# Two instruction streams in a fixed TensorE order for the token mixing of a hybrid decoder

## The chip, the cores and the metric

The kernel runs on one core of one Trainium2 chip. The metric is the device time of one execution in microseconds: 3290.15 us is the median of three runs of the kernel before (3289.18 to 3293.43). The engines are PE (TensorE), DVE (VectorE), ACT (ScalarE), POOL (GpSimd) and SP (SyncE, which issues DMAs).

## The reference

One step of a decoder of two layers for 512 prompt tokens and 8 sample sequences of 8 tokens, 576 tokens in all, width 1024. All in fp32. Cut to what matters:

```
def run_trunk(x, ...):
    for l in range(DEPTH):                       # 2 layers
        x = layer_norm(ALPHA*x + 0.5*swiglu(x, ffn1_w_in, ffn1_w_out))
        mix, st = token_mixing(x, ...)
        x = layer_norm(ALPHA*x + mix)
        x = layer_norm(ALPHA*x + 0.5*swiglu(x, ffn2_w_in, ffn2_w_out))

def token_mixing(h, ...):
    pa, pb, pc, pm, pg = split(h @ w_in)         # one input projection for all branches
    oa = rwkv7_branch(pa)        # 8 heads x 64: a state per head, updated token by token
    ob = pool_branch(pb)         # causal windows of 2, 4, 8, 16
    oc = delta_branch(pc)        # 4 heads x 128: gated delta rule in chunks of 64 tokens
    om = memory_attention(pm)    # 256 memory tokens
    gates = sigmoid(pg)          # 4 x 1024
    merged = sum_i gates_i * (o_i @ w_branch_i)
    return merged @ w_out

# delta rule, by chunk of 64 tokens (the kernel brings the rwkv rule to the same form):
tmat = inverse(eye + strict_lower(...))          # unit triangular, 64 x 64
def step(s, ...):                                # one chunk after another
    v_new = u_i - w_i @ s
    o = qd_i @ s + a_i @ v_new
    s = s * exp(gl_i) + kd_i.T @ v_new
```

## The kernel before

**Dense products.** Features lie on the partitions, tokens on the free axis, in two halves of 288. A weight block of 128 columns is loaded raw by SP's DMA queue, cast to fp32r by ACT (line 232, the high part) and the rest taken by DVE (line 234, the low part); a product of one 128x128 block with 288 tokens is three matmuls (high-high, low-high, high-low, line 248). Eight blocks give 24 matmuls into one PSUM tile. `ffn` does only such products. PSUM tiles of dense products have two buffers each of tags `mm` and `mg` and one of `mf`; all small products use three buffers of the pool `pb`.

**Mixing.** Each layer runs four rwkv pairs of heads (p = 0 to 3, `rwkv_prep`, `rwkv_chain`, `rwkv_out`), then two delta pairs (q = 0, 1, `delta_pair`). A pair has a *preparation* (projections; elementwise work on DVE and ACT; token-by-token matrices `pt` or `pdm` on PE), an *inverse* (`inverse64`: 31 columns of two DVE instructions each, lines 614 and 616, after a transpose at line 608 and before two at 621 and 627; PE then multiplies in `py` and `pd`; the sample group's 8x8 blocks by seven steps `px`) and a *chain* of eight chunks. A rwkv chunk is `pr` on PE, `rhs` on DVE, `psa` on PE, `VS` on ACT, `pu` on PE, `S` on DVE, and the next chunk needs `S`; `pyc` is the output. A delta chunk is `pdk` and `pdq`, `drhs`, `pdz`, `z`, `pdo` and `pdu`, `S`. The sample group has steps of its own, in rwkv laid between the chunks, in delta after them.

**What sets the order.** Every engine runs its instructions in one order, which a list scheduler sets before the run from the program's order and its costs. Dense work that no chain needs yet (pooling, attention, gates `pgt` and branch products `pbr`) is the generator `fill_steps`; `advance` takes steps of it at places given by `ORDER`, `PLAN`, `RWKV_EVERY` and `DELTA_EVERY`, and the scheduler then moves pieces of it into the gaps of PE. It does so matmul by matmul:

```
            if k % self.tk == self.tk - 1 and self.started:
                self.advance(self.fill_gen, 1)
```

stands between the columns of the inverse.

Of the kernel before, what the change touches and what calls it, by code (L numbers as in the profile page):

```python
# [8 lines left out]
F32 = mybir.dt.float32  # L9
# [6 lines left out]
P = 128  # L16
D = 1024
DEPTH = 2
SEQ = 512
NS = 8          # sample sequences  # L20
LS = 8          # tokens of each
# [4 lines left out]
NC_ = 9         # chunks of 64 tokens: 8 of the prompt, one of the sample group  # L26
# [24 lines left out]
# rows of 128 parameters, in two groups that one transpose each brings onto the partitions  # L51
# [4 lines left out]

# how the work that fills the tensor engine's gaps in the token mixing is laid between the rest: its order at first
# (P: pooling and attention, G: gates of the first merge), how many steps of it go where, and how many columns of an
# inverse lie between two steps
ORDER = "P" * 11 + "GP" * 16  # L60
PLAN = (12, 0, 4, 0, 12, 8, 0, 0, 2, 0, 4, 4, 0, 2)
RWKV_EVERY, DELTA_EVERY = 3, 8


class Decoder:
    def __init__(self, tc, ctx, ins, outs):
# [12 lines left out]
        self.ptag = "mm"  # L79
        self.norm = None  # L80
        self.started = False
# [10 lines left out]
    def dense(self, tag, name):  # L92
        return self.pm.tile([P, HT], F32, tag=tag, name=name)

    def fill(self, name):
        return self.pm.tile([P, 512], F32, tag="mg", name=name)
# [14 lines left out]
    def tri(self, t, strict, block=None):  # L111
        """t[s, j] (square in the last two dims of a [n, n] tile): 1 where s <= j (s < j if strict) else 0."""
# [5 lines left out]
    def blockdiag(self, t, b):  # L118
        """zero outside the b x b diagonal blocks of t [n, m]."""
# [8 lines left out]
    def constants(self):  # L128
# [11 lines left out]
        # inclusive upper triangles, by chunk of 64 and by sequence of 8  # L140
# [6 lines left out]
        # seqmask[t, b] = 1 where token t (mod 64) belongs to sequence b  # L147
# [3 lines left out]
        # masks of the RWKV token x token matrices [s | s, t strict | t inclusive]  # L151
# [10 lines left out]
        # 0 where s <= t else NEG: [128 = (h, s), 2 kinds, 64]  # L162
# [17 lines left out]
        # 0 at the first token of a chunk or sequence, else 1  # L180
# [6 lines left out]
        # 1 / (t + 1)  # L187
# [170 lines left out]
    def out_norm(self, units, X, which, lag, ahead, final=False):  # L358
# [7 lines left out]
        def step(i, s):  # L366
# [4 lines left out]
            if kh == 0:  # L371
                ps[s] = self.dense(("mm", "mg")[s], "po")
# [461 lines left out]
    def rwkv_chain(self, l, p, parts):  # L834
# [33 lines left out]
        for _ in sample:  # L868
            pass
# [736 lines left out]
```

## Time and profile before

| | |
|---|---|
| median of three runs | 3290.15 us |
| span of the profiled execution | 3291.1 us |
| PE busy | 3164.5 us, 96% |
| PE weight loads busy | 2886.2 us, 88% |
| DVE busy | 1896.7 us, 58% |
| ACT busy | 1276.8 us, 39% |
| POOL busy | 581.2 us, 18% |

The profiled execution lies within 1 us of the median, so its span can stand for the time. A matmul record begins when the array takes the instruction, and its modelled end reaches into the next ones, so a busy PE is not a PE that does useful work all the time: a record is also lengthened while the array changes from one tile shape to another. The shape stands in the timeline's rows: `128*128` is a product that uses all rows and columns of the array, `64*64`, `128*64` or `32*32` one that uses a part. Waits of PE are listed by what ended them.

### The profile page before, as it was taken

What the parts mean: (1) busy time and instruction counts of PE and PEld (TensorE: products, weight loads), DVE (VectorE), ACT (ScalarE), POOL (GpSimd) and SP (SyncE); (2) the same over time, 40 slices, a digit from 0 to 9 for tenths busy, and PEclk for the clock granted to TensorE, in tenths of its full rate; (3) what the DMA queues carried; (4) which work ended last, traced back from release to release, by engine and by line L of the source; (5) the groups of instructions that cost most, each with busy time, mean ns of one, the idle gap of its engine ahead of it and who ended that gap; (6) DMA issues with size and microseconds to landing.
All of it is one profiled execution on the core that took longest, in us unless ns stands there. A gap on an engine that the chain in (4) does not pass through costs nothing. (4 is left out here: it accounts for less than half of the span.)

```text
span 3291.1 us, 62683 instructions
## 1 busy us (share of the span) xinstructions
PE 3164.5 (96%) x24736; PEld 2886.2 (88%) x24736; DVE 1896.7 (58%) x4205; ACT 1276.8 (39%) x3015; POOL 581.2 (18%) x898
## 2 busy tenths in 40 slices
PE   7999999999999999999999999998999999999998
PEld 7999887688888799999999998776888797989998
DVE  5336676465677656733663376675475786475336
ACT  4323544434434233432343244444345342343324
POOL 2002311111110014400330032111111100152004
PEclk8999899999999899999999999999999998999999
DMA  4223331142233233332333232312322232323222
GB/s 137 80 84 96 87 111 44 41 118 55 60 83 78 57 105 91 91 87 80 88 103 87 81 107 72 105 51 55 102 58 61 67 99 64 98 85 97 84 81 77
DMA packets 509908, 271.96 MB, mean 83 GB/s; under 512 B 45897, under 2 KB 500141, under 8 KB 509613
## 3 DMA queue, kind: packets, MB, share of 16 engines
q1 hardware_dynamic: 509612, 267.95, 29.0%
q8 instruction: 194, 3.18, 0.4%
q14 instruction: 102, 0.83, 0.1%
HBM read 248.12 MB, written 19.76 MB: 81 GB/s over the span
## 5 line engine op out<-in xcount | busy, mean ns | idle before, releaser
L234 DVE TENSOR_TENSOR w<-raw,w 128x512 fp32r<-128x512 f32 (+1 forms) x824 | 604.7, 739 | 385.2 <-ACT w L232 378.0
L232 ACT CAST w<-raw 128x512 fp32r<-128x512 f32 (+1 forms) x824 | 501.6, 615 | 608.8 <-PE po L248 236.4
L248 PE MATMUL pp<-X,w 128*128 128x288 f32 x3552 | 550.9, 307 | 11.1 <-DVE X L262 5.5
L248 PEld LDWEIGHTS pp<-X,w 128*128 128x128 f32 x3552 | 495.1, 193 | 40.1 <-issue 15.3
L248 PE MATMUL pgt<-X,w 128*128 128x288 f32 x3072 | 500.9, 309 | 5.1 <-ACT th__12080 L1484 2.1
L248 PEld LDWEIGHTS pgt<-X,w 128*128 128x128 f32 x3072 | 435.1, 193 | 32.6 <-issue 13.9
L248 PE MATMUL pg<-X,w 128*128 128x288 f32 x3072 | 441.8, 297 | 10.2 <-DVE X L262 6.1
L248 PE MATMUL pu<-X,w 128*128 128x288 f32 x3072 | 437.4, 297 | 0.0
L248 PEld LDWEIGHTS pg<-X,w 128*128 128x128 f32 x3072 | 419.7, 189 | 15.7 <-DVE X L262 9.6
L248 PEld LDWEIGHTS pu<-X,w 128*128 128x128 f32 x3072 | 420.9, 190 | 0.6
L248 PE MATMUL po<-H,w 128*128 128x288 f32 x3072 | 413.9, 296 | 0.0
L248 PEld LDWEIGHTS po<-H,w 128*128 128x128 f32 x3072 | 409.4, 188 | 1.3
L248 PE MATMUL pbr<-O,w 128*128 128x288 f32 x1344 | 227.6, 308 | 12.9 <-ACT w L232 4.1
L248 PEld LDWEIGHTS pbr<-O,w 128*128 128x128 f32 x1344 | 190.9, 191 | 27.9 <-issue 7.3
L276 POOL TENSOR_TENSOR T<-T,m 128x288 f32<-128x288 f32 x48 | 48.0, 1029 | 925.7 <-ACT m L297 925.4
L433 DVE TENSOR_TENSOR h<-h,pu 128x288 f32<-128x288 f32 x128 | 58.0, 453 | 259.2 <-PE pu L248 259.1
L261 ACT CAST H<-h 128x288 fp32r<-128x288 f32 x128 | 55.2, 431 | 189.5 <-DVE h L433 189.4
L432 ACT ACTIVATE h<-pg 128x288 f32<-128x288 f32 x128 | 52.7, 411 | 172.8 <-PE pg L248 172.8
L248 PE MATMUL po<-mh,w 128*128 128x288 f32 x768 | 109.0, 302 | 9.2 <-DVE T L281 9.2
L248 PEld LDWEIGHTS po<-mh,w 128*128 128x128 f32 x768 | 105.6, 193 | 11.4 <-DVE T L281 6.9
L614 DVE TENSOR_TENSOR it<-W,iu 128x60 f32<-128x60 f32 (+24 forms) x372 | 97.7, 263 | 9.2
L353 POOL TENSOR_TENSOR T<-T,off 128x288 f32<-128x288 f32 x96 | 83.4, 900 | 91.5 <-ACT off L348 65.0
(1018 smaller groups left out, 3747.8 us busy)
## 6 DMA issues: line engine op xcount, KB each, us to landing
raw<-in_w_in_dram SPq DMA_DIRECT2D x280, 256.0 KB
raw<-in_ffn_w_in_dram SPq DMA_DIRECT2D x272, 256.0 KB
raw<-in_ffn_w_out_dram SPq DMA_DIRECT2D x160, 256.0 KB
raw<-in_w_branch_dram SPq DMA_DIRECT2D x48, 256.0 KB
raw<-in_w_out_dram SPq DMA_DIRECT2D x48, 256.0 KB
oraw<-od SPq DMA_DIRECT2D x28, 288.0 KB
kraw<-in_mem_w_kv_dram SPq DMA_DIRECT2D x16, 256.0 KB
kvr<-in_cache_mem_k_dram SPq DMA_DIRECT2D x16, 256.0 KB
```

What stands on the lines that cost most here:

```text
L232: nc.scalar.copy(w[:, 0, :m], raw)
L234: low.tensor_sub(w[:, 1, :m], raw, w[:, 0, :m].bitcast(F32))
L248: self.nc.tensor.matmul(ps, w[:, wp, d, :], X[k][:, part, sl], start=first and k == 0 and q == 0, stop=last and k == n - 1 and q == 2)
L261: nc.scalar.copy(out[:, 0, sl], src)
L276: nc.gpsimd.tensor_sub(t, t, self.stat[s]['m'])
L353: nc.gpsimd.tensor_add(T[j], T[j], off)
L432: nc.scalar.activation(h, pg, AF.Silu)
L433: nc.vector.tensor_mul(h, h, pu)
L614: nc.vector.tensor_mul(w, d[:, :r, k:k + 1].to_broadcast([P, r, m]), u[:, k + 1:, k].unsqueeze(1).to_broadcast([P, r, m]))
```

## The change

The order of PE in the mixing is written out by hand (`manual_schedule` for PE alone); DVE, ACT and POOL are still ordered by the scheduler. Preparation, inverse and chain are generators now that yield at the places where PE would wait; the number that they yield is a credit in matmuls, and `feed` takes dense work for it in pieces of twelve matmuls (`mms_steps`), the next pair's projections or the delta gates first (`urgent`). A credit of 8 stands for one hop of a chain, 2 x 8, 7 x 8 and 5 x 8 for longer waits; what a piece takes too much is taken off the next credit.

In the chain, products of one tile shape stand together: `pyc`'s part with the state comes with `pr`, its other part with `pu`, the own-chunk output `pdo` of delta one chunk later with the next `pdz`; the sample group's steps are put beside chunks' products of their own shape (`wide`, `solve`, `deep`; `state`, `solve`, `update`). The 8x8 inverse takes four steps of six products in place of seven steps. Attention's softmax runs two behind its scores, the two halves of `rwkv_out` go together, the delta gates are projected during the inverse, fill weights use the tag `wm` alone, and all dense PSUM tiles have one tag of four banks.

```diff
-ORDER = "P" * 11 + "GP" * 16
-PLAN = (12, 0, 4, 0, 12, 8, 0, 0, 2, 0, 4, 4, 0, 2)
-RWKV_EVERY, DELTA_EVERY = 3, 8
+HOP = 8
+COLUMNS = 2
+PIECE = 12
...
-        self.pm = pool("pm", 2, space=ps)
+        self.pm = pool("pm", 4, space=ps)
...
+    def mms_steps(self, ps, unit, X, sl, then):
+        n, per = len(unit), PIECE // 3
+        for k in range(0, n, per):
+            m = min(n, k + per)
+            self.mms(ps, unit[k:m], X[k:m], sl, k == 0, m == n)
+            if m == n:
+                then()
+            yield 3 * (m - k)
...
     def inverse64(self, U, at):
...
+        last = self.inverse8(U, at, W)
         for k in range(31):
...
-            if k % self.tk == self.tk - 1 and self.started:
-                self.advance(self.fill_gen, 1)
+            if k % COLUMNS == COLUMNS - 1:
+                if k % (2 * COLUMNS) == COLUMNS - 1:
+                    next(last, None)
+                yield HOP - 1
...
-        for k in range(7):
-            px = self.bank("px")
-            for h in range(2):
-                r = slice(at(h), at(h) + 64)
-                a, b = (U(h)[:, 8], x[r]) if k < 6 else (x[r], U(h)[:, 8])
-                nc.tensor.matmul(px[r, :64], a, b, start=True, stop=True)
-            x = self.scr.tile([P, 64], F32, tag="r64", name="ix", bufs=3) if k < 6 else W[:, 8]
-            nc.vector.tensor_sub(x, self.id2, px[:, :64])
...
+    def inverse8(self, U, at, W):
...
+        ps = products("px", (u, on(self.id2)))
+        nc.scalar.copy(a, ps[:, :64])
+        nc.vector.tensor_sub(b, self.id2, ps[:, :64])
+        yield
+        ps = products("px2", (on(a), u), (u, on(a)))
+        nc.scalar.copy(c, ps[:, :P])
+        nc.vector.tensor_add(a, self.id2, ps[:, :64])
+        yield
+        ps = products("px3", (on(b), on(a)), (on(c[:, 0:64]), on(c[:, 64:128])))
+        nc.vector.tensor_copy(w[:, 0:128], ps[:, :P])
+        yield
+        ps = products("px4", (on(b), on(a)))
+        nc.vector.tensor_add(W[:, 8], a, ps[:, :64])
+        yield
...
     def rwkv_prep(self, l, p, front, wx, lr):
...
+        yield 2 * HOP
         for sl in HALVES:
             ps = self.bank("pss")
...
+        yield 7 * HOP
         MA = [self.slot(f"MA{h}", F32, [P, NC_, 2, 64]) for h in range(2)]
...
     def rwkv_chain(self, l, p, parts):
...
+            if S is not None:
+                for h in range(2):
+                    nc.tensor.matmul(py[R[h], :64], S[R[h]], KR[R[h], c, 1], start=True, stop=False)
             nc.vector.tensor_copy(rhs, pr[:, :64])
+            sample_step("wide")
+            yield HOP
             self.rwkv_solve(parts, c, rhs)
-            py, pu = self.bank("pyc"), self.bank("pu")
+            sample_step("solve")
+            yield HOP
+            pu = self.bank("pu")
...
-                if S is not None:
-                    nc.tensor.matmul(py[R[h], :64], S[R[h]], KR[R[h], c, 1], start=True, stop=False)
...
-            next(sample, None)
-        for _ in sample:
-            pass
+            sample_step("deep")
+            yield HOP
...
     def delta_pair(self, l, q, sc):
...
-        self.advance(self.fill_gen, PLAN[8 + 3 * q])
+        yield 2 * HOP
...
+        yield HOP
         for c0, m in ((0, 5), (5, 4)):
             pd = self.bank("pdec")
...
+        yield 2 * HOP
         MA = self.slot("dMA", F32, [P, NC_, 2, 64])
...
+            if c % 3 == 2:
+                yield HOP
...
-        self.advance(self.fill_gen, PLAN[9 + 3 * q])
-        self.tk = DELTA_EVERY
-        DT = self.inverse64(lambda h: MA[R[h], :, 0], lambda h: 64 * h)
+        self.urgent = gates()
+        DT = yield from self.inverse64(lambda h: MA[R[h], :, 0], lambda h: 64 * h)
...
+        yield 5 * HOP
         for c0 in range(0, NC_, 4):
             pt = self.bank("pto")
...
-    def advance(self, steps, n):
-        for _ in range(n):
-            self.started = True
-            if next(steps, self) is self:
+    def feed(self, want):
+        self.credit += want
+        while self.credit > 0:
+            n = None
+            if self.urgent:
+                n = next(self.urgent, None)
+                if n is None:
+                    self.urgent = None
+            if n is None:
+                n = next(self.dense_work, None)
+            if n is None:
+                self.credit = 0
                 return
+            self.credit -= abs(n)
...
     def mixing(self, l):
...
-        self.advance(fill, 1000)
+        with self.tc.manual_schedule(engines={mybir.EngineType.PE}):
+            for want in work:
+                self.feed(want)
+            for _ in self.dense_work:
+                pass
```

Three places of PE's order follow; in a row stand the line, the operation, the tile written and the tiles read, the shape of the result and how many stand together. Line 248 before is line 250 after.

PE before, one rwkv chunk of the first pair (`pp` is dense work, `psa` the solve, `pu` the state's update, `pyc` the output; `S` is the state):

```order
L846 MATMUL pr<-S_5498,KR 64x64
L847 MATMUL pr<-VS,MA_4377 64x64
L846 MATMUL pr<-S_5498,KR 64x64
L847 MATMUL pr<-VS,MA_4378 64x64
L248 MATMUL pp<-X,w 128x288 x3
L830 MATMUL psa<-rhs,W 64x64 x2
L248 MATMUL pp<-X,w 128x288 x3
L854 MATMUL pu<-VS,KN 64x64 x2
L858 MATMUL pyc<-KR,S_5498 64x64
L859 MATMUL pyc<-MA_4377,VS 64x64
L858 MATMUL pyc<-KR,S_5498 64x64
L859 MATMUL pyc<-MA_4378,VS 64x64
```

PE after, a chunk of the same chain:

```order
L250 MATMUL pp<-X,w 128x288 x12
L911 MATMUL pr<-S_5173,KR 64x64
L912 MATMUL pr<-VS,MA_4484 64x64
L911 MATMUL pr<-S_5173,KR 64x64
L912 MATMUL pr<-VS,MA_4485 64x64
L916 MATMUL pyc<-KR,S_5173 64x64 x2
...
L250 MATMUL pp<-X,w 128x288 x12
L886 MATMUL psa<-rhs,W 64x64 x2
L886 MATMUL psa<-r_5205,W 64x64 x2
L926 MATMUL pu<-VS,KN 64x64 x2
L929 MATMUL pyc<-MA_4484,VS 64x64
L929 MATMUL pyc<-MA_4485,VS 64x64
```

Twelve dense matmuls stand ahead of `psa` and ahead of the next `pr`, where three stood; between `psa` and `pu` stood three, and nothing but a sample step's `psa` stands there now; `pyc` with the state has moved up to `pr`. Over the whole program the dense runs are 596 before and 370 after, counted in this order.

PE before, preparation of the first pair, from the last projection of the decay (`pz`, `pa`) over the norms (`pss`) to the matrices (`pt`):

```order
L248 MATMUL pp<-X,w 128x288 x8
L740 MATMUL pa<-wx,lr 128x288
L248 MATMUL pp<-X,w 128x288 x32
L758 MATMUL pss<-yg,b_94 128x288 x2
L248 MATMUL pp<-X,w 128x288 x39
L1298 MATMUL ppool<-pbo,pw 128x288 x2
L248 MATMUL pp<-X,w 128x288
...
L248 MATMUL pp<-X,w 128x288 x34
L786 MATMUL pt_4379<-KR,KB 128x128 x4
```

PE after, the same stretch:

```order
L792 MATMUL pa<-wx,lr 128x288
L250 MATMUL pp<-X,w 128x288 x24
L804 MATMUL pss<-yg,b_94 128x288 x2
L250 MATMUL pp<-X,w 128x288 x48
L837 MATMUL pt_4486<-KR,KB 128x128 x4
```

Between `pa` and `pt` stood 109 dense matmuls, and 72 stand there now.

PE before, preparation of the first delta pair, from the transposes of queries and keys (`ptq`, `ptk`) on:

```order
L1098 MATMUL ptk_10002<-ident,dk 128x128
L248 MATMUL pgt<-X,w 128x288 x22
L248 MATMUL pbr<-O,w 128x288 x6
L248 MATMUL pp<-X,w 128x288
L248 MATMUL pgt<-X,w 128x288 x2
L1106 MATMUL ptv_10020<-ident,dv 128x128 x4
L1097 MATMUL ptq<-ident,dq 128x128 x2
```

PE after, the end of the same transposes and the way to the matrices (`pdm`):

```order
L1187 MATMUL ptk_9822<-ident,dk 128x128
L1195 MATMUL ptv_9828<-ident,dv 128x128
L250 MATMUL pgt<-X,w 128x288 x12
L1217 MATMUL pdec<-dec,b_94 128x320
L1217 MATMUL pdec<-dec,b_94 128x256
L250 MATMUL pgt<-X,w 128x288 x12
L1230 MATMUL pdm<-dk 64x64
```

From the first `ptq` to the first `pdm` stood 55 dense matmuls and stand 24; they have gone from between the transposes. From the last `pt` or `pdm` to the first `py` of an inverse, the six pairs of a layer had 132, 113, 79, 179, 178 and 160 of them (841) and have 96, 108, 72, 48, 108 and 108 (540), beside other fill work.

## Rows read from the trace of the kernel before

**Rows 1.** The page: span, busy time of engines, granted clock by slice.

```profile
span 3291.1 us, 62683 instructions
...
PE 3164.5 (96%) x24736; PEld 2886.2 (88%) x24736; DVE 1896.7 (58%) x4205; ACT 1276.8 (39%) x3015; POOL 581.2 (18%) x898
...
PEclk8999899999999899999999999999999998999999
```

**Rows 2.** Waits of PE: us in total, times, longest.

```profile
PE ppt L1397 <- DVE prob L1318: 14.1, 6, 5.9
...
PE py L635 <- DVE iy L621: 7.4, 3, 3.6
...
PE pt L786 <- DVE KB L773: 2.9, 2, 1.5
```

**Rows 3.** Chain of waits, in order of time: start us, us, what.

```profile
2844.07 3.20 PE pgt L248 x24
```

**Rows 4.** Timeline of PE, one rwkv chunk: start us, us, what, count.

```profile
506.29 0.33 PE L830 MATMUL psa<-rhs,W 64*64 64x64 f32 x4
506.55 0.67 PE L248 MATMUL pp<-X,w 128*128 128x288 f32 x3
507.15 0.36 PE L854 MATMUL pu<-VS,KN 128*64 128x64 f32 x4
507.44 0.33 PE L858 MATMUL pyc<-KR,S 64*64 64x64 f32 x2
507.70 0.33 PE L859 MATMUL pyc<-MA,VS 128*64 128x64 f32 x2
```

**Rows 5.** Timeline of ACT, the same chunk.

```profile
506.67 0.46 ACT L832 ACTIVATE VS<-psa 64x64 f32<-64x64 f32 x2 [2.30 <-PE psa L830]
```

**Rows 6.** Timeline of PE, preparation of the second rwkv pair.

```profile
526.05 0.75 PE L740 MATMUL pa<-wx,lr 64*128 64x288 f32 x2
...
532.08 1.24 PE L758 MATMUL pss<-yg,b 128*128 128x288 f32 x4
...
537.75 5.84 PE L248 MATMUL pp<-X,w 128*128 128x288 f32 x42
545.04 1.92 PE L786 MATMUL pt<-KR,KB 64*128 64x128 f32 x14 [1.45 <-DVE KB L773]
```

**Rows 7.** Timeline of DVE, the same stretch.

```profile
528.08 1.40 DVE L744 TENSOR_TENSOR_SCAN e<-cont,e 128x256 f32<-128x256 f32 x2
...
534.32 3.74 DVE L760 RECIPROCAL yg<-yg 128x576 f32<-128x576 f32 x1
...
544.25 1.53 DVE L773 TENSOR_TENSOR KB<-pa,e 64x576 f32<-64x576 f32 x2
```

**Rows 8.** Groups by line, DVE, the inverses: busy us, mean ns; idle.

```profile
L614 DVE TENSOR_TENSOR it<-W,iu 128x60 f32<-128x60 f32 (+24 forms) x372 | 97.7, 263 | 9.2
L616 DVE TENSOR_TENSOR W<-W,it 128x60 f32<-128x60 f32 (+24 forms) x372 | 82.8, 223 | 9.1
```

**Rows 9.** Timeline of DVE, the inverse of the second rwkv pair.

```profile
553.40 1.97 DVE L608 STREAM_TRANSPOSE iu<-cp 128x1024 f32<-128x1024 f32 x1
...
574.96 0.65 DVE L621 STREAM_TRANSPOSE iy<-W 128x256 f32<-128x256 f32 x1
575.64 1.80 DVE L627 STREAM_TRANSPOSE W<-iy 32x256 f32<-32x256 f32 x4
```

**Rows 10.** Timeline of PE, first delta pair's preparation.

```profile
902.99 0.27 PE L1097 MATMUL ptq<-ident,dq 128*128 128x128 f32 x1
```

**Rows 11.** Timeline of DVE, the same preparation.

```profile
922.31 0.35 DVE L1140 SCALAR_TENSOR_TENSOR dMA<-pdm,dcs,dec 128x128 f32<-128x128 f32 x1
```

**Rows 12.** Timeline of PE, third rwkv pair's preparation: the long wait.

```profile
658.02 0.48 PE L1397 MATMUL ppt<-ident,prob 128*128 128x128 f32 x1 [5.88 <-DVE prob L1318]
658.15 4.19 PE L248 MATMUL pgt<-X,w 128*128 128x288 f32 x16
```

**Rows 13.** Stretches: us, busy of PE, PEld, DVE, ACT, POOL, granted clock.

```profile
655.00:662.00 7.00, 3.98 (x17) 3.97 (x17) 6.97 (x12) 0.00 (x0) 0.00 (x0) 0.55 0.15 42
```

More of the change, by code (lines that the diff above doesn't have):

```diff
@@ L953, in rwkv_out, with rwkv @@
             self.stash(p, y, sl)
-    def rwkv(self, l, fill=None):
+        yield HOP
+    def rwkv(self, l):
         wx, lr, front = self.rwkv_common(l)
-        front = self.rwkv_front(l, 0, front)
+        front, steps = self.rwkv_front(l, 0, front)
+        for _ in steps:
+            pass
         self.sc = self.delta_scalars(l)
+        yield 0
         for p in range(4):
-            parts = self.rwkv_prep(l, p, front, wx, lr)
-            self.advance(fill, PLAN[2 * p])
+            parts = yield from self.rwkv_prep(l, p, front, wx, lr)
@@ L1163, in delta_pair, with sample_step @@
+        group = sample()
+        wanted = next(group)
+        def sample_step(kind):
+            nonlocal wanted
+            if wanted == kind:
+                wanted = next(group, None)
         S = [None, None]
-        for c in range(8):
-            if c:
+        before = None
+        for c in range(9):
+            if 0 < c < 8:
                 pk, pq = self.bank("pdk"), self.bank("pdq")
@@ L1267, in pool @@
             for k in ((0, 1), (2,), (3,), ())[j]:
-                rows(k)
-                yield
+                yield from rows(k)
             w = 2 << j
@@ L1381, in attention, with scores @@
         nc.scalar.copy(KT, pt.rearrange("p (q m) -> p q m", q=2))
+        yield -4
+        PT, po, behind = {}, {}, []
+        def scores(p, h, g):
+            ps = self.fill("psc")
+            for d in range(2):
+                t = (2 * g + d) * P
+                nc.tensor.matmul(ps[:, d * 256:(d + 1) * 256], Q[R[h], p, t:t + P], KT[R[h], p],
+                                 start=True, stop=True)
+            pr = tile("prob", [P, 2, 256])
+            self.softmax(ps.rearrange("p (k m) -> p k m", k=2), pr)
+            behind.append((p, h, g, pr))
@@ new lines, in transposed @@
+        def transposed():
+            p, h, g, pr = behind.pop(0)
+            if g == 0:
+                PT[p, h] = tile("PT", [P, 2, 512])
+            pt = self.fill("ppt")
+            for m in range(2):
+                for d in range(2):
+                    nc.tensor.transpose(pt[:, (2 * m + d) * P:(2 * m + d + 1) * P], pr[:, d, m * P:(m + 1) * P],
+                                        self.ident)
+            nc.scalar.copy(PT[p, h][:, :, g * 256:(g + 1) * 256], pt.rearrange("p (m t) -> p m t", m=2))
+            return p, h, g
@@ L1494, in early @@
                     for s in range(2):
[L1495 to L1509 removed]
+                        yield from gate(j, s, self.M[j // 2][:, j % 2, HALVES[s]])
+            early = early()
+            for k in first:
+                yield abs(k)
+                if k < 0:
+                    yield next(early, 0)
+            yield from early
         for j in range(8):
[L1511 to L1513 removed]
+            if first is None:
+                for s in range(2):
+                    yield from gate(j, s, self.half("th_", "xf"))
             if j == 0:
```

462 lines of the change are left out of this document (257 added, 205 removed).

## The prediction

> **What bounds the kernel now.** I read the page first: PE is busy for 3164.5 of 3291.1 us, DVE for 58% of it [rows 1]. So PE bounds the kernel, and what is not useful on PE is of three kinds: idle time (3291.1 - 3164.5 = 126.6 us), stretches at half clock (the 8 and 9 tenths in the clock's line [rows 1]), and the time in which the array changes between tile shapes, which counts as busy. The list of waits comes next: the largest in the mixing are waits for softmax, inverse and preparation on DVE, and none is a DMA [rows 2]. The longest single wait, 5.9 us, stands where the order had put a transpose of the attention in front of the dense work [rows 2, 12]. The chain of waits gives the price of dense work: 24 matmuls in 3.20 us, 0.133 us each [rows 3]. The timeline of one rwkv chunk shows the third kind [rows 4]: three dense matmuls between `psa` and `pu` are worth 0.40 us by that price, and from `psa` to `pu` go 507.15 - 506.29 = 0.86 us. The rest, 0.46 us, is the way out of the small shape and back, with the issue of four `psa` in it. From `pu` over the first `pyc` to the second stand 0.29 and 0.26 us for four and two matmuls of 64 columns, a step each time that the shape changes.
>
> **What it removes.** The count of matmuls hardly changes; the dense runs fall from 596 to 370. Each run costs the way in and out once. Seen from the dense run alone (506.55 to 507.15, less 0.40) it is 0.20 us, with `psa` 0.46 us [rows 4]; I take 0.35, since most of the 0.46 is not the issue of four matmuls. 226 runs fewer give 79 us (45 to 104). In the chunk, `pu`, `pyc`, `pyc`, `pyc`, `pyc` change the shape four times before; after it `pr` and `pyc` with the state have one shape, `psa` too, and `pu` with the other `pyc` one. Three steps of 0.26 us in 56 of 64 chunks (the first of a chain has no state) are 44 us [rows 4]; the matmuls themselves still issue, and the bare `psa` to `pu` is a new change, so I take 30 (0 to 44). The 8x8 inverse has four steps in place of seven; its returns are in the 226. Of the idle 126.6 us [rows 1] about 55 go, since all waits in the mixing are counted anew below; three of them alone are 14.1 + 7.4 + 2.9 = 24 us [rows 2], so 24 to 80. Together 164 us (69 to 228).
>
> **What it adds: waits at places where the cover is smaller than the chain beside it.** The order of PE is fixed either way; what counts is how much work stands between the two ends of each dependency. Behind an instruction that waits, all dense work waits too.
>
> *Preparation, rwkv.* From `pa` at 526.05 [rows 6] DVE does scan, reciprocal (3.74 us alone) and products until `KB` ends at 544.25 + 1.53 = 545.78 [rows 7]: 19.7 us, with a few weights' and softmax instructions of other work between, so some 16.5 of its own. After, PE has between the same ends 72 x 0.133 = 9.6 us of dense work, `pss` 1.24, `pa` 0.75 [rows 6] and two returns of 0.35: 12.3 us for the first pair. (The second and third pairs have fewer dense matmuls and other fill in their place, near the same sum; the fourth has more.) The wait is 4.2 to 7.4 us; I take 6 for three pairs and 2 for the fourth, 20 a layer, 40 us in all (26 to 55). Before, 109 dense matmuls covered it to 2.9 us in all [rows 2].
>
> *Inverse.* The columns cost (97.7 + 82.8) / 12 = 15.0 us on DVE [rows 8], and the transposes 1.97 + 0.65 + 1.80 [rows 9]: 19.5 us bare. With other DVE work between it took 577.44 - 553.40 = 24.0 us in the trace [rows 9]. PE's cover falls from 841 dense matmuls a layer to 540, or from 18.6 to 12.0 us for one inverse; with the other fill, transposes and returns beside them I put it at 19 us. So the wait at `py` is 0.5 us if DVE does nothing else, 5 us if it does what it did; the changed DVE order has as much other work there as before, and for the first pair more (the pooling sums). I take 5.5 for each of twelve, 66 us (6 to 100). This is the largest and least certain term. In the trace of before it is 7.4 [rows 2], already taken off.
>
> *Hops without work.* A credit of 8 paid by pieces of 12 leaves each third hop bare, and in 46 of 64 chunks it is the one from `psa` to `pu`. There ACT's two instructions run from 506.67 to 507.13, 0.38 after `psa` starts [rows 5]; `pu` starts at 507.15. Of the 0.86 us about 0.2 is PE's own issue and a change of shape, so a bare hop idles 0.65 us: 30 us (20 to 40). For the bare hops elsewhere (`pu` to `pr`, `pdz` to `pdu`) I take 0.4 us at about 45 places, 18 us (0 to 30), each being shorter by what PE issues in it.
>
> *Preparation, delta.* From the first `ptq` at 902.99 [rows 10] to the first `dMA` at 922.31 [rows 11] ACT and DVE need 19.3 us, of which 3 or 4 are weights and merge. PE had 55 dense matmuls up to `pdm`. After it has 24 (3.2 us), 27 transposes, `pdec` and two returns, 8 to 9 us. The wait is 8 to 11 us; four times 10.5 are 42 us (28 to 46). For the norm ahead of `pto`, where 48 dense matmuls (6.4 us) stand beside a like series of ACT instructions, I take 3 us each, 12 us (0 to 25).
>
> Together 40 + 66 + 30 + 18 + 42 + 12 = 208 us (80 to 296).
>
> One PSUM tag of four banks in place of two of two has the same room; fill weights on `wm` alone have four buffers, and the dense runs in which they are used are not longer, so both are at 0 (-5 to +10: if a low part's subtraction queues on DVE behind columns of the inverse, dense work waits for it, as a `pbr` would). The half clock of before stays in the sum. Outside the mixing nothing changes.
>
> **Sum.** 3291.1 - 164 + 208 = 3335 us for the profiled execution, which stands 1 us above the median; I predict 3335. What the hops don't use of the dense work isn't lost: it runs after the last chain without waits, but it can't cover anything there.
>
> **The rivals.**
>
> *The cover is enough, faster.* If DVE does the chain's instructions first and the other work afterwards, each chain has its bare length: preparation 26, inverse 6, hops 20 + 18, delta 28, norm 12, together 110 us, and 3291 - 164 + 110 = 3237 us. For it: DVE has 42% of its time free [rows 1], and in the inverse of the trace its columns run nearly without a gap (9.2 us idle ahead of 372 instructions [rows 8]). Against it: the same rows show weights between columns, and the weights of dense work can't be put off for long. It is faster from the point where the waits fall below 164 us.
>
> *Gain and waits cancel.* Within 0.2% (6.6 us, about what a measurement of this kernel tells from no change) the waits must be between 157 and 171 us. Nothing draws them there; it would be 3290.
>
> *The waits also take the clock, slower still.* After the wait of 5.88 us in the trace, 16 dense matmuls took 4.19 us, where 16 x 0.133 are 2.13 [rows 12], and the stretch had a granted clock of 0.55, between 1.2 and 2.4 GHz [rows 13]: 2.1 us on top of the wait. The new waits of five microseconds and more number 12 at inverses, 6 to 8 at preparations and 4 at delta preparations. With 2.1 us for each of 24, the time is 3335 + 50 = 3385 us. Against it: short waits with dense runs around them need not fall under this, and the waits of before had it in the sum already. It decides if most waits exceed 5 us.
>
> The Trainium skill has this as a rule (TensorE: Matmul & The Clock Gate, section "HAM oscillation — how this bites in real kernels"): a loop of short matmul bursts parted by waits lets the clock fall to half before each next burst, so that the price is paid each time. The stretch of 0.55 agrees with it here [rows 13]; by that rule the last rival holds, and this is why it has a chance of its own.
>
> **How the numbers follow.** Forecast (3300 to 3360) 0.44; faster (3200 to 3283) 0.33; cancelled 0.06; slower with the clock (3360 to 3400) 0.17. Slower by over 0.2% is 0.44 + 0.17 = 0.61, the same 0.06, faster 0.33. The sum's bounds alone go from 3291 - 228 + 80 = 3143 to 3291 - 69 + 296 = 3518, but all terms won't go to one end. I take 3215 to 3395, which leaves out the better third of the faster case and the tail of the slower one, about 2 in 10. The likeliest case alone is 3300 to 3360.
>
> **What would show it.** In the changed profile PE's idle time should rise from 127 to about 280 us and its records shorten; the list of waits should be led by `py` for `iy` or `W` (66), `pt` for `KB` (40), `pdm` or its neighbours for ACT and DVE of the delta preparation, and `pu` for `VS` (30, some 0.65 us each). The dense matmuls in the chains should come twelve at a time in 1.6 us. The forecast is wrong if PE's idle time stays under 230 us; then the inverse's cover is the first term to look at. It is also wrong if the way in and out of a small shape still costs as much in sum as before, which the mean time of `pp` and `pgt` records would show.

## The result and the profile after

The changed kernel is slower: 3431.97 us median (3430.23 to 3433.62) against 3291.71 of the kernel before beside it, a ratio of 1.0424 (95% interval 1.0411 to 1.0437). It lies beyond the range and beyond the dearest rival (3385). The profiled execution has a span of 3428.5 us.

The page after has the lines that answer to [rows 1]:

```profile
span 3428.5 us, 62462 instructions
...
PE 3128.1 (91%) x24688; PEld 2893.9 (84%) x24688; DVE 1880.8 (55%) x4169; ACT 1286.0 (38%) x3039; POOL 567.2 (17%) x898
...
PEclk9999889998999999999999998999899999999999
```

PE's idle time went from 126.6 to 3428.5 - 3128.1 = 300.4 us, that is 174 more, and its busy time fell by 36 only. The line of the clock has whole tenths and hides what the mean granted clock shows, in the first line before, in the second after:

```profile
core 0: 3291.1 us, clock 0.974
core 0: 3428.5 us, clock 0.952
```

So at 1.2 GHz in place of 2.4 the kernel before spent 2 x 0.026 x 3291 = 171 us and the one after 2 x 0.048 x 3428 = 329 us. Of the waits in PE's list these are the larger ones in the mixing (us in total, times, longest); [rows 2] has three of them before:

```profile
PE py L657 <- DVE iy L643: 39.8, 8, 8.5
PE pu L926 <- ACT VS L888: 23.7, 46, 1.8
PE ppt L1609 <- DVE prob L1450: 21.8, 4, 8.2
PE ptl L607 <- POOL tl L588: 15.7, 22, 1.0
...
PE pt L837 <- DVE KB L823: 14.4, 4, 5.1
PE pa L792 <- DVE yg L1033: 11.8, 6, 3.3
PE pcum L1110 <- DVE dsc L1104: 10.8, 2, 5.4
PE pto L1381 <- DVE dON L1375: 9.4, 4, 2.8
...
PE ptv L1195 <- DVE dv L1160: 8.9, 4, 2.2
PE pkv L1480 <- DVE wkv L1475: 8.5, 2, 4.3
PE pdk L1328 <- DVE dS L1354: 7.6, 4, 1.9
```

The inverse is the largest, as forecast, but at 39.8 us and not at 66; most of the forecast terms came out smaller. A long series of small waits, at places that the sum did not price, makes up the rest. PE in a rwkv chunk after, which answers to [rows 4]:

```profile
494.96 1.86 PE L250 MATMUL pp<-X,w 128*128 128x288 f32 x12
496.75 0.33 PE L886 MATMUL psa<-rhs,W 64*64 64x64 f32 x4
497.77 0.51 PE L926 MATMUL pu<-VS,KN 128*64 128x64 f32 x3 [0.69 <-ACT VS L888]
498.02 0.27 PE L929 MATMUL pyc<-MA,VS 128*64 128x64 f32 x1
```

Twelve dense matmuls take 1.8 us, and the bare hop idles 0.69 us. The preparation of the first pair, for [rows 6], and the first delta inverse, on PE and then on DVE, for [rows 9]:

```profile
407.04 4.93 PE L250 MATMUL pp<-X,w 128*128 128x288 f32 x24
411.81 1.13 PE L804 MATMUL pss<-yg,b 128*128 128x288 f32 x4
412.56 6.74 PE L250 MATMUL pp<-X,w 128*128 128x288 f32 x48
424.41 1.86 PE L837 MATMUL pt<-KR,KB 64*128 64x128 f32 x9 [5.11 <-DVE KB L823]
...
967.49 1.74 PE L250 MATMUL pgt<-X,w 128*128 128x288 f32 x12
975.86 1.06 PE L657 MATMUL py<-iy,dMA 32*32 32x32 f32 x32 [6.63 <-DVE iy L643]
976.85 3.25 PE L250 MATMUL pgt<-X,w 128*128 128x288 f32 x12
```

```profile
953.57 2.02 DVE L627 STREAM_TRANSPOSE iu<-cp 128x1024 f32<-128x1024 f32 x1 [1.19 <-ACT cp L625]
...
975.10 0.61 DVE L643 STREAM_TRANSPOSE iy<-W 128x256 f32<-128x256 f32 x1
```

In both places the dense work is used up long before DVE has done. After the wait of 6.63 us twelve matmuls take 3.25 us, where 12 x 0.133 are 1.6: the stretch ran at a lower clock (columns: us, busy of PE, PEld, DVE, ACT and POOL, granted clock, DMA share, GB/s):

```profile
973.00:985.00 12.00, 8.23 (x95) 7.28 (x96) 5.29 (x18) 2.36 (x6) 0.61 (x2) 0.67 0.29 78
768.00:786.00 18.00, 12.27 (x65) 12.04 (x65) 8.53 (x14) 1.70 (x6) 0.00 (x0) 0.53 0.09 29
```

The second is the wait of 8.2 us for softmax at `ppt`.

**An account of the difference.** For each step from one matmul to the next I took the median time that a step between the same two shapes takes at full clock in the trace of before, and summed it over PE's order of each kernel: the *issue*. What the trace has above that is either in stretches at half clock (the *half clock*) or in *waits*. Us, from the profiled executions; the dense runs are counted in PE's order:

| kernel | issue | half clock | waits | dense runs | median |
|---|---|---|---|---|---|
| before | 3095 | 72 | 117 | 596 | 3290 |
| after | 2989 | 135 | 297 | 370 | 3432 |

By this account the change saves 106 us of issue and pays 180 in waits and 63 in clock for it: -106 + 180 + 63 = +137, and the spans differ by 137.4. The three sums are an account, not a measurement, and another choice of what a normal step is shifts tens of us between them. What the traces give without it is the idle time, 174 us more, and the stretch at half clock, 171 us before and 329 after. The runs below test the rest.

### The profile page after: what moved, and what is told of

It is laid out like the page before. It is cut to its first block, busy times and chain, and to the rows that moved or that the text cites. A ratio compares the mean times of both kernels' runs of the same rounds, so it can differ in the third digit from the quotient of the medians.

```text
span 3428.5 us, 62462 instructions
## 1 busy us (share of the span) xinstructions
PE 3128.1 (91%) x24688; PEld 2893.9 (84%) x24688; DVE 1880.8 (55%) x4169; ACT 1286.0 (38%) x3039; POOL 567.2 (17%) x898
## 4 chain that ended last, share of the span: by engine, by line
PE 64%; DVE 13%; ACT 4%; issue 2%; POOL 1%; DMA 1%; SPq 0%; DVEq 0%; POOLq 0%; ACTq 0%
PE pgt L250 10%; PE pp L250 10%; PE po L250 9%; PE pu L250 8%; PE pg L250 8%; PE pbr L250 5%; DVE w L236 1%; DVE it L634 1%; DVE W L636 1%; PE pu L926 1%; POOL T L365 1%; ACT w L234 1%; DVE X L274 1%; PE pt L837 1%; DVE yg L806 1%
## 5 line engine op out<-in xcount | busy, mean ns | idle before, releaser
L250 PE MATMUL pp<-X,w 128*128 128x288 f32 x3552 | 526.4, 304 | 5.3 <-DVE X L274 4.8
L250 PE MATMUL pgt<-X,w 128*128 128x288 f32 x3072 | 473.5, 310 | 0.0
L250 PEld LDWEIGHTS pg<-X,w 128*128 128x128 f32 x3072 | 418.1, 188 | 15.7 <-DVE X L274 11.8
L250 PE MATMUL pbr<-O,w 128*128 128x288 f32 x1344 | 205.0, 305 | 6.7 <-ACT w L234 4.8
L286 POOL TENSOR_TENSOR T<-X 128x288 f32<-128x288 f32 x96 | 93.8, 1010 | 35.5 <-DVE X L484 23.3
```

The costliest lines, as they stand in the source:

```text
L250: self.nc.tensor.matmul(ps, w[:, wp, d, :], X[k][:, part, sl], start=first and k == 0 and q == 0, stop=last and k == n - 1 and q == 2)
L286: nc.gpsimd.tensor_add(t, self.X[j][:, 0, sl].bitcast(F32), self.X[j][:, 1, sl].bitcast(F32))
```

## The experiments

The medians in one group were taken beside runs of the kernel before, which had 3293 to 3294. Theories: A, the waits come from a fixed order that can't be filled and from cover laid in the wrong places, and the clock falls with them; rivals as each expectation names them. Cover is the dense work that PE does while it would else wait; the stock is all that there is of it. Comments in the code cuts are added here. First the changed kernel with PE's order left to the scheduler:

```diff
-        with self.tc.manual_schedule(engines={mybir.EngineType.PE}):
-            for want in work:
-                self.feed(want)
-            for _ in self.dense_work:
-                pass
+        for want in work:
+            self.feed(want)
+        for _ in self.dense_work:
+            pass
```

> The changed kernel with one part undone: PE's order in the mixing is left to the scheduler again, the program text is the same. Theory A (the waits come from too little cover, and the hand-written order forbids to fill them): the scheduler pulls three to six dense matmuls into the bare hops from psa to pu and some in front of other waits; PE's idle time falls from 300 us by about the 24 us of these hops and some 20 us more, the half clock by 30 us of stretch or so, and the time is 3430 - 60 = 3370 us. Rival B (the program's order of preparation, chain and fill sets the waits, whoever writes it down): within 15 us of 3432.

Measured 3294.06 us, ratio 0.9999 (0.9986 to 1.0012): the fixed order costs 138 us, as much as the whole loss and more than either theory said. By the account issue is 3026, half clock 111, waits 155.

Dense work taken earlier, order fixed:

```diff
-                yield HOP - 1
+                yield HOP - 1 + self.more        # 4 in the first rwkv and both delta inverses
...
-        yield 7 * HOP
+        yield 7 * HOP + (36, 0, 16, 0)[p]
...
-        self.sc = self.delta_scalars(l)
         yield 0
+        self.sc = yield from self.delta_scalars(l)     # with 4 * HOP ahead of pcum
...
```

> The changed kernel with more dense work (no work added, only taken earlier) at the places of the longest waits: 4 matmuls more per two columns in the first rwkv inverse and both delta inverses, 36 and 16 more ahead of pt in the first and third pair, 32 ahead of pcum (with the delta scalars brought into the fixed order), 16 and 16 more ahead of the delta transposes and pdm, 16 ahead of pto, 8 after rwkv_out, three more gate pieces ahead of the samples' softmax transposes. Theory A (waits plus the clock that they take): about 350 matmuls a layer cover up to 45 us of idle time a layer, and half clock falls by 100 us of stretch, so 3432 - 90 - 40 = 3300 us (3270 to 3350). Rival B (idle time alone, clock unrelated): 3340. Rival C (the waits move on, because DVE's other work comes with the dense work: its weights' low parts queue between the columns): 3400 or more.

3382.5 us, 1.0272 (1.0255 to 1.0289): 50 us back, where A said 132 and B 92; the time lies between B and C. The waits at `py` fell from 39.8 to 14.9 and those at `pcum` went, but the wait of `ppool` for `pbo` rose from 2.6 to 14.4 and that of `pa` from 11.8 to 14.7. That waits move on is what C says; that the weights' low parts on DVE are the reason isn't shown.

Throwaway matmuls in the waits:

```diff
+    def keep_busy(self, n):
+        if n:
+            ps = self.dense("dm")
+            for k in range(n):
+                self.nc.tensor.matmul(ps, self.X[0][:, 0, 0:P], self.X[1][:, 0, HALVES[0]], start=k == 0, stop=k == n - 1)
...
                 yield HOP - 1
+        self.keep_busy(self.idle)     # 24 or 40 ahead of py
```

> The changed kernel with throwaway dense matmuls (results never read) issued just ahead of the longest waits, sized to fit in them: 40 before py of the delta inverses, 24 before py of the first rwkv inverse, 32 and 12 before pt of the first and third pair, 40 and 16 before the samples' softmax transposes. They move no useful work. Theory A (half clock after long waits is a cost of its own): the half-clock stretches at these places go, about 100 us of 328, and the time falls by 25 to 45 us though more is computed. Rival B (only the waits cost): unchanged or up to 15 us slower.

3420.58 us, 1.0382 (1.0367 to 1.0398): 11 us faster with 408 matmuls more. The half clock fell by 48 us of stretch (clock 0.952 to 0.959). More work in less time speaks for a price of the clock apart from the waits, and against B; the gain is less than A's 25 to 45, with half of the 100 us of stretch that A had.

The kernel before with `pyc` regrouped alone:

```diff
+            if S is not None:
+                for h in range(2):
+                    nc.tensor.matmul(py[R[h], :64], S[R[h]], KR[R[h], c, 1], start=True, stop=False)
             nc.vector.tensor_copy(rhs, pr[:, :64])
             self.rwkv_solve(parts, c, rhs)
...
-                if S is not None:
-                    nc.tensor.matmul(py[R[h], :64], S[R[h]], KR[R[h], c, 1], start=True, stop=False)
                 nc.tensor.matmul(py[R[h], :64], vs, MA[h][:, c, 1], start=S is None, stop=True)
```

> The kernel before with one part of the change alone: in the rwkv chain the two products of pyc with the state stand next to pr, and the two with VS next to pu; all else, the scheduler included, is as before. Theory A (each change of tile shape costs a step of about 0.26 us): three steps fewer in 56 chunks, 30 to 44 us faster, so 3250 to 3262. Rival B (the steps lie in the wait for S or are paid back as waits of the chain, whose length rises by the matmuls put ahead of psa): within 10 us of before.

3249.52 us, 0.9873 (0.9846 to 0.99): 44 us faster, the upper bound of A. The chunk two ahead of that of [rows 4] takes 501.87 - 498.28 = 3.59 us from `psa` to the next `psa` in the kernel before, with seven dense matmuls in it:

```profile
498.28 0.33 PE L830 MATMUL psa<-rhs,W 64*64 64x64 f32 x4
...
501.87 0.33 PE L830 MATMUL psa<-rhs,W 64*64 64x64 f32 x4
```

In this run the same chunk, with seven as well, takes 498.58 - 495.89 = 2.69 us, and `pyc` stands in one row 0.16 us behind `pu`:

```profile
495.89 0.33 PE L830 MATMUL psa<-rhs,W 64*64 64x64 f32 x4
496.15 0.66 PE L248 MATMUL pp<-X,w 128*128 128x288 f32 x3
496.75 0.36 PE L857 MATMUL pu<-VS,KN 128*64 128x64 f32 x4
496.91 0.32 PE L860 MATMUL pyc<-MA,VS 128*64 128x64 f32 x4
...
498.58 0.33 PE L830 MATMUL psa<-rhs,W 64*64 64x64 f32 x4
```

The account gives it 3053 of issue (-42), 69 of half clock and 113 of waits: here the issue sum is borne out by a time.

All regroupings in the kernel before (`pdo` one chunk later, and the change's `inverse8` with `next(last, None)` in every fourth column in place of the seven steps), and the same with the old 8x8 inverse:

```diff
-                z, po = tokens(c, rhs)
-                nc.vector.tensor_add(ON[:, c], ON[:, c], po[:, :P])
+                z = tokens(c, rhs)
+                po = own(c - 1, last)
+                if c == 1:
+                    nc.vector.tensor_copy(ON[:, 0], po[:, :P])
+                else:
+                    nc.vector.tensor_add(ON[:, c - 1], ON[:, c - 1], po[:, :P])
...
+        last = self.inverse8(U, at, W)
         for k in range(31):
             r, m = k // 4 + 1, 31 - k
+            if k % 4 == 1:
+                next(last, None)
```

> The kernel before with the change's regroupings alone, without the two streams, the credits or the fixed order: pyc next to pr and pu, delta's pdo one chunk later next to the next pdz, and the 8x8 inverse in four steps beside the columns. Theory A (each step between tile shapes costs 0.2 to 0.3 us, wherever it stands): 28 delta chunks save some 0.3 us each and the doubling some 1 us in 12 inverses, so 15 to 25 us under the run with pyc alone (3250): 3225 to 3237. Rival B (pdo's wait was hidden, and the doubling moves DVE work between the columns of the inverse, which lengthens it by 4 instructions of about 0.2 us each): 3245 to 3260.

> As the run with all regroupings, but with the seven steps of the 8x8 inverse as before: pyc and pdo regrouped. Theory A: about 8 us under the run with pyc alone, near 3240, with the doubling's part as the rest of the difference. Rival B: the same as pyc alone, 3250.

3232.87 us, 0.9817 (0.9802 to 0.9831), and 3242.9, 0.9849 (0.9835 to 0.9864). In steps from 3293: `pyc` -44, `pdo` about -7, the 8x8 inverse in four steps -10. The step of `pdo` isn't clear of noise, since the intervals with and without it (0.9846 to 0.99, 0.9835 to 0.9864) overlap; the sum of 60 is. Issue 3041, half clock 63, waits 121: the grouping costs nothing elsewhere. So by the account 54 of the 106 us of issue are the grouping's, for free, and 52 are left for dense runs: this run has 606 of them and the changed kernel 370, which makes 0.22 us for each of 236. No run tests this last price by itself.

The changed kernel with the first two edits together (scheduled, added cover); and with the order fixed in the chains alone (`fixed` is set ahead of `rwkv_chain` and of the delta chain, and taken back after them; the cut is against the scheduled run):

```diff
         for want in work:
             self.feed(want)
+            if self.fixed:
+                with self.tc.manual_schedule(engines={mybir.EngineType.PE}):
+                    for want in work:
+                        self.feed(want)
+                        if not self.fixed:
+                            break
```

> The changed kernel with PE's order left to the scheduler, as in the run that took back the fixed order, and with the added cover of the run that took dense work earlier. Theory A (two causes that add: places that the fixed order can't fill, and too small credits at the inverse and the preparation): the waits at pt for KB (37 us) and py for iy (33 us) of the scheduled run fall by half, the half clock by 50 us of stretch, and the time is 3294 - 35 - 20 = 3240 us (3225 to 3265). Rival B (the scheduler pulls dense work ahead into earlier gaps whatever the credits say, so that it is gone where the chain waits): within 15 us of 3294.

> The changed kernel with PE's order fixed in the chains alone (rwkv_chain with rwkv_out left out, and the delta chain), and left to the scheduler in preparations, inverses and between. Theory A (the fixed order costs most in preparation, inverse, attention and pooling, where a dozen kinds of short waits stand, and in the chains only the bare hops, 24 us at pu and some 20 at pdk, pdu and pr): 3294 + 45 + a little half clock = 3340 to 3355 us. Rival B (the chains' bare hops are most of it): over 3385. Rival C (fixing the chains costs nothing against the scheduler): within 15 us of 3294.

3334.0 us, 1.0125 (1.011 to 1.0141): A and B both fell; it is 40 us *slower* than without the cover. The wait at `py` fell from 32.7 to 18.3, but that at `pt` only from 37.1 to 34.3, and the mean granted clock went from 0.959 to 0.954. 3375.97 us, 1.0256 (1.0239 to 1.0273): fixing the chains alone costs 82 of the 138 us, between A and B. But not by bare hops (`pu` for `VS` 10 us), which was B's reason: the wait at the inverses was the first of these in the scheduled run and is the second here:

```profile
PE py L657 <- DVE iy L643: 32.7, 10, 6.2
PE py L658 <- DVE iy L644: 72.5, 10, 13.6
```

A reading of this is that a chain that takes 24 dense matmuls in a chunk, where the kernel before put three at a hop, uses up what the inverse would need. To test it the stock was laid out otherwise, order fixed (the second run has the first edit, `PIECE = 3`, alone):

```diff
-PIECE = 12
+PIECE = 3
+CHAIN = 4
...
-            yield HOP
+            yield CHAIN                     # all hops of both chains
...
-        yield 7 * HOP
+        yield 7 * HOP + (54, 24, 36, 16)[p]
+        self.more = (8, 5, 5, 5)[p]         # in the inverses; 8 in delta's
```

> The changed kernel, fixed order kept, with the dense work laid out otherwise: pieces of 3, a credit of 4 (not 8) for each hop of a chain, and the matmuls that this frees, with some 330 a layer of those left over at the end, laid at the inverses (4 to 8 more per two columns), ahead of pt (16 to 54 more), pcum, the delta transposes, pdm and pto. Theory A (the chains take three to four times the dense work that their hops need, and preparations and inverses starve for it): PE's waits fall from 300 us to 180, half clock by 80 us of stretch, and shorter dense runs cost some 50 us more issue, so 3432 - 120 - 35 + 50 = 3325 us (3300 to 3350). Rival B (what the fixed order can't do is follow the times of DVE, wherever the work is laid): waits stay above 240 us and the time above 3400.

> The changed kernel with PIECE = 3 in place of 12 and nothing else: a credit of 8 is paid by 9, 9 or 6 matmuls at every hop, so that none is bare, with the same amount of work in sum. Theory A (bare hops are a small part of the loss): the waits of pu for VS (24 us) and some 15 us of pdu, pdk and pr go; the dense runs rise by about a hundred, which costs 0.22 us each, so 3432 - 39 + 22 = 3415 us. Rival B (the bare hops and the clock that they take are the loss): under 3380.

3353.0 us, 1.0179 (1.016 to 1.0198), and 3398.93, 1.0316 (1.03 to 1.0332). With the stock moved, `py` for `iy` and `pt` for `KB` are gone from the list and the waits are 184 us by the account, near A's 180; B falls. The time lies 3 us above A's range, and one part of A fell: the stretch at half clock lost 14 us, not 80. What is left above the old kernel is the clock (137 in the account) and small waits:

```profile
PE ptl L609 <- POOL tl L590: 22.7, 24, 1.6
PE prow L359 <- DVE dg L355: 17.0, 8, 4.9
PE ppool L1435 <- DVE pbo L1430: 14.8, 2, 7.4
```

Smaller pieces alone (the second run) gain 33 us, twice the 17 that A said and less than B's 52; the wait of `pu` for `VS` is gone from the head of its list.

One PSUM tag of four in the regrouped old kernel, and four gate pieces after each step of the attention and pooling in the run before:

```diff
-        self.pm = pool("pm", 2, space=ps)
+        self.pm = pool("pm", 4, space=ps)
...
     def dense(self, tag, name):
-        return self.pm.tile([P, HT], F32, tag=tag, name=name)
+        return self.pm.tile([P, 512], F32, tag="mm", name=name)[:, :HT]
...
     def fill(self, name):
-        return self.pm.tile([P, 512], F32, tag="mg", name=name)
+        return self.pm.tile([P, 512], F32, tag="mm", name=name)
```

```diff
                 if k < 0:
-                    yield next(early, 0)
+                    for _ in range(4):
+                        yield next(early, 0)
```

> The run with all regroupings (the kernel before with pyc, pdo and the 8x8 inverse changed), and beside it the change's PSUM layout: one tag of four banks for all dense products and fill tiles, in place of two tags of two. Theory A (the room is the same, and no wait of PE in the trace is for a free bank): within 6 us of 3233. Rival B (fill and dense tiles, which had banks of their own, now hold each other up, so that the tag is a part of what the two-stream version lost): 3250 or more.

> The run with the dense work laid out otherwise (fixed order, pieces of 3, hops of 4), with one thing mended: after each step of the attention and the pooling four pieces of 3 of a gate's product follow, where the smaller piece had left one. The amount of work is the same. Theory A (the clock falls where small products or waits stand together with little dense work between, as in its stretch from 550 to 570 us): half clock falls by 50 us of stretch or more, waits for softmax by 8 us, and the time is 3353 - 30 = 3323 us (3305 to 3335). Rival B (the clock's loss doesn't hang on how the small products are spread): within 8 us of 3353.

3427.3 us, 1.0398 (1.038 to 1.0416): the tag alone costs 194 us, so B holds and A fell. The half clock is at 200 in the account, and the wait at the inverse is the second of these, where it was the first with two tags:

```profile
PE py L638 <- DVE iy L624: 17.1, 5, 4.4
PE py L638 <- DVE iy L624: 41.2, 8, 11.7
```

3331.4 us, 1.0105 (1.0083 to 1.0127) for the gates: 22 us, the half clock 51 us of stretch less (314 to 263). The first two lines are of the run before it, the last two of this one:

```profile
PE 3144.9 (94%) x24688; PEld 2883.4 (86%) x24688; DVE 1888.4 (56%) x4169; ACT 1284.3 (38%) x3039; POOL 577.7 (17%) x898
core 0: 3351.8 us, clock 0.953
...
PE 3124.0 (94%) x24688; PEld 2868.4 (86%) x24688; DVE 1885.2 (57%) x4169; ACT 1282.8 (39%) x3039; POOL 582.0 (17%) x898
core 0: 3330.1 us, clock 0.961
```

PE's idle time is the same in both, 3351.8 - 3144.9 = 206.9 and 3330.1 - 3124.0 = 206.1 us, and the waits for softmax did not fall by the 8 us that A had. So the whole gain is in busy time, and the clock is what changed: spreading the small products among dense work raises it, as A said.

That left open what the tag does to the changed kernel:

```diff
-    def dense(self, name):
-        return self.pm.tile([P, 512], F32, tag="mm", name=name)[:, :HT]
+    def dense(self, name, second=False):
+        tag = "mg" if second or name in ("pu", "pgt", "pbr") else "mm"
+        return self.pm.tile([P, 512], F32, tag=tag, name=name)[:, :HT]
```

(fill tiles on `mg`, two banks each; under the fixed order `pgt` and `pbr` stay on `mm`.)

> The changed kernel, fixed order kept, with two tags of two banks (dense products on one, fill tiles and pu of the feed-forward on the other) in place of one of four. Theory A (under a fixed order, banks are taken in the order in which PE uses them, so the tag costs nothing there): 3432 within 15 us, or slower since each stream has two banks instead of four. Rival B (the tag is a part of the 140 us): under 3400.

> The changed kernel with PE's order left to the scheduler, and two tags of two banks as in the kernel before (gates, branch products and fill tiles on the second). Theory A (banks are given out in the program's order, so with one tag the scheduler can't take fill work ahead of the chain's own dense work; with two it can): waits of PE fall from 155 to 125 us and half clock from 274 to under 200 us of stretch, time 3294 - 30 - 35 = 3230 us, like the regroupings alone (3233). Rival B (the tag matters only for the old program): 3294 within 15 us.

> The run with the dense work laid out otherwise and the gates mended (3331 us under the fixed order), with PE left to the scheduler and two tags of two banks. Theory A: the scheduler fills what is left and the layout gives it enough ahead of preparations and inverses, 3215 to 3235 us, the lowest of the two-stream programs. Rival B (the layout moves work away from where the scheduler would use it, as the added cover did with one tag: 3334 against 3294): 3250 or more.

3467.34 us, 1.0521 (1.0506 to 1.0537); 3261.89, 0.9903 (0.9889 to 0.9918); 3226.52, 0.9795 (0.9779 to 0.9812). In the first B falls; A had left open that it could be slower, and it is, by 35 us. In the second the tag gives 32 us, so B falls, but A had said twice as much. In the third A holds. This is the fastest of all runs, 68 us under the old kernel:

```profile
PE 3100.1 (96%) x24688; PEld 2844.1 (88%) x24688; DVE 1879.5 (58%) x4169; ACT 1279.5 (40%) x3039; POOL 571.5 (18%) x898
...
core 0: 3220.9 us, clock 0.981
```

But it is only 6 us under the regroupings alone (3232.87), and the two intervals (0.9779 to 0.9812, 0.9802 to 0.9831) overlap: no run shows that two streams gain anything beyond the regroupings.

| two-stream program | one tag of four | two tags of two |
|---|---|---|
| fixed order | 3432 | 3467 |
| scheduled | 3294 | 3262 |
| fixed, stock laid out anew, gates spread | 3331 | not tried |
| scheduled, stock laid out anew, gates spread | not tried | 3227 |

## Why the prediction was wrong

The direction was right, and so was the mechanism of steps and waits: the matmul steps were saved, and waits where the cover is smaller than the chain took more than that. What the new order does to the clock was left out. The size was wrong by 93 us, +137 against +44. By the account 63 of them are clock, 27 waits (180 against 208 - 55 = 153) and 3 steps (106 against 109).

**The step that failed** is "The half clock of before stays in the sum", which put the change of the clock at nothing. It was 63 us more in the account. Two runs price it without the account: 22 us for 51 us of stretch with the gates spread, 11 for 48 with throwaway matmuls. At these prices the 329 - 171 = 158 us more of stretch are about 67 and 37 us. The rival with the clock had the right mechanism, but priced 24 long waits alone (50 us); the clock also fell where small products stood together without dense work. That spreading gates between them brought 51 us of stretch back with the idle time unchanged shows this; how the 63 us divide between waits and bunched products is open. Two terms of the sum failed beside it, and are below: waits at places that it did not price, and the PSUM tag, put at nothing. The Trainium skill's rule (TensorE: Matmul & The Clock Gate, section "HAM oscillation — how this bites in real kernels"), that bursts parted by waits pay for the clock anew, agrees with the stretches at 0.67 and 0.53 above.

**What the change removes** was right in sum (109 forecast for steps, 106 in the account) by luck, since two errors cancel: by the account a dense run less is 0.22 us, not 0.35 (52, not 79), and the regroupings are 54 to 60, not 30 plus nothing for the others. The regroupings were timed alone, at -44, -7 and -10; the dense runs were not. PE's busy time fell by 36 us, and with 37 to 67 us of clock in it the saving is 73 to 103 us, so the 106, and the 52 in it, may be somewhat high. The sign that the prediction named for it, the mean time of `pp` and `pgt` records, does not decide: 307 and 309 ns before, 304 and 310 after, with more of them at half clock. The Trainium skill says that a change of tiling mode drains the engine (TensorEngine Tiling (Array Packing), section "Key Properties"); the timelines agree, with 3.59 us for the chunk before and 2.69 with `pyc` grouped. The prediction counted three changes fewer in a chunk; the rows show four, between `pu` and the end of `pyc`, so the 44 us in 56 chunks are 0.20 us for each, not 0.26.

**What it adds.** Idle time rose by 174 us, where 153 were forecast, and to 300 where 280 were. Term by term, by the list of waits: bare hops at `pu` 23.7 (forecast 30), `pto` 9.4 (12), `py` 39.8 and the preparation 14.4 (66 and 40, too dear: only 8 waits at `py` for 12 inverses and 4 at `pt` for 8 pairs), `ptv` and its neighbours of the delta preparation about 27 (42), `pdk`, `pdu` and `pr` 14 (18 for the other bare hops). Against that, `ppt`, `ptl`, `pa`, `pcum` and `pkv` have 69 us, and were not in the sum at all (`ppt` and `ptl` had some 20 before). So the total came near by luck: terms that were too dear made up for places left out. The places that were priced are mostly those where the program yields; the waits stood also where it does not.

**The tag.** That one tag "has the same room" put it at nothing. Under the fixed order it is worth 35 us: two tags are that much slower there. With the scheduler it costs 194 us in the old program and 32 in the new. The prices are measured; the reason is only argued, from the orders: banks are given out in the program's order, so with one tag the scheduler can't take fill work ahead of a chain's own dense tile, or leave it behind. Undoing both the fixed order and the one tag gives 170 us.

**The rival "the cover is enough"** failed for want of a stock laid where the long chains are: with it laid there, the waits of `py` for `iy` and of `pt` for `KB` do vanish under the fixed order too, and 79 us with them (101 with the gates spread).

## What to carry to other kernels

Count how much dense work there is to hide chains behind, and lay it by the length of each chain: hops of 0.6 us need three or four matmuls, an inverse of 24 us some 180 at 0.133 us each. Take the part of a rewrite that only puts products of one tile shape next to each other by itself first: here it gave 60 us alone, the rewrite around it lost 200, and the best of its mended versions was 6 us better than the regroupings, which is within the noise. Before writing an order by hand, run the same program with the scheduler's: here this one edit gave back the 138 us.

## What was not expected of the hardware

The clock fell also without any wait. In the kernel before, PE is busy all the time from 396.5 to 409.8 us: up to 403 with the end of a dense run, the delta scalars (`pcum`, `pgl`, products of one to eight columns) and projections of the decay, then mostly with dense matmuls. And yet the granted clock goes from full to half (columns as above):

```profile
396.50:403.00 6.50, 6.50 (x58) 6.12 (x56) 2.56 (x14) 2.87 (x7) 0.00 (x0) 1.00 0.08 15
403.00:409.80 6.80, 6.80 (x24) 5.26 (x23) 1.52 (x3) 3.43 (x10) 1.22 (x2) 0.50 0.08 25
```

So fewer waits need not mean more clock: in the run with the stock laid out anew PE's idle time was 300 - 207 = 93 us less than after, and the half-clock stretch only 14 us less (0.953 against 0.952), until dense work was put between the attention's small products (0.961). And the waits for POOL's copies of tails (`ptl`), 5.4 us before, were 22.7 in that run: no engine's share on the page (POOL 17%) hints at them.
